# Modulation weights of the first norm in five groups instead of six, in one transformer-like layer on one core

## The chip, the cores and the metric

The kernel runs on one core of a Trainium2 chip. The metric is the device time of one execution in microseconds (us), lower is better. The kernel before takes 958.6 us, the median of three runs (958.38 to 959.06).

Engines are named as in the profile: PE (TensorE, matmuls; PEld is its weight load), DVE (VectorE), ACT (ScalarE), POOL (GpSimd) and SP (SyncE, which here only issues DMAs). A trailing q, as in SPq, means the engine's sequencer.

## The reference, cut to what matters

The program is one layer of a diffusion backbone in fp32: 512 latent tokens `x` and 256 context tokens `ctx`, width 1024. The layer's norms are modulated: a vector computed from the conditioning input `c` (for `x`) or `c_ctx` (for `ctx`) scales and shifts each of the 1024 channels.

```
sh1x, sc1x, ... = split(silu(c)     @ w_ada + b_ada, 6)
sh1c, sc1c, ... = split(silu(c_ctx) @ w_ada + b_ada, 6)
hc = rms_norm(ctx, norm1_g) * (1 + sc1c) + sh1c
hx = rms_norm(x,   norm1_g) * (1 + sc1x) + sh1x
z  = hx @ w_in                       # u, vs, q, r, ga, gb, k, v, lr
...
```

From `z` follow a spatial gating branch, a gated linear attention in both directions over the tokens, whose start states come from `hc`, a merge of both, and a convolutional feed-forward part with a second modulated norm. Only the beginning matters here: the shift and scale of the first norm (the first 2048 of the 6144 columns of `w_ada`, 8 MB), the normalised and modulated `hx`, and the first products with `w_in`.

## The kernel before

**Layout and number format.** The 1024 channels are eight tiles of 128, with the channel on the partition. Large products take an fp32 operand as two fp32r parts, a high part (`h`) and the remainder (`l`), and add three matmuls: high by high, high by low, low by high.

**The interleaved beginning.** At the start all data come from memory at once, and the kernel weaves three things together over the eight channel tiles k (the loop at L587):

- *The modulation.* The tiles are cut into groups: `GROUPS = (1, 1, 1, 1, 2, 2)` at L200, with `G0` the first tile of each. For a group, `ada_load(g)` (L210) loads the columns of `w_ada` for shift and scale as 256 KB transfers into tiles named `wa`: a one-tile group takes 4 of them, with 128 columns (512 B) in a run, a two-tile group 8, with 256 columns (1 KB) in a run. `ada_dot(g)` (L446, its matmuls at L455) multiplies them with the two activated condition vectors, 16 matmuls whatever the group's width, whose result DVE copies to `asb` (L602). `ada_sel(g)` (L459) turns the result to one column per channel with one small matmul per tile (L464) and makes scale `am` and shift `bm` with three short DVE operations (L467 to L469). `ada_mod(g)` (L471) applies them to the tiles of the group (L478) and splits each into `hxh` and `hxl`.
- *The first products.* `first_step(i, k, z)` (L523, matmul at L531): six outputs (q, k and four token tiles of v) times three part products, 18 matmuls per tile k. They need `hx[k]` and the rows of `w_in` that `first_load(i)` (L222) brings for two tiles at a time, 512 KB for v into a `raw` tile and two times 128 KB for q and k into `qkraw`. `first_split(i)` (L439) splits these: ACT casts the high parts (L441), DVE subtracts (L442). `first_split(1)` stands at the head of step k = 1, `first_split(2)` and `(3)` inside `ada_mod`, at tiles 4 and 6.
- *Small work*: after step 2 a transpose of `rows_b` to `vec_b` (L342) and `w2_stack` (L563, L566, L567), four DVE operations; after steps 3 and 7 a narrow product with `w_lr` (L513).

**Where the groups stand.** In the last step of a group's tiles the next group is made ready. The table `AT` (L586) gives, by the current group, before which third of the step's 18 matmuls `ada_dot` of the next group is issued; `ada_sel` and `ada_mod` follow one third later. With `AT = {0: 1, 1: 0, 2: 0, 3: 1, 4: 0}` the groups 1 to 5 are prepared in the steps 0, 1, 2, 3 and 5.

**What sets the order.** `in_order(START, nc.sync.engine)` (L241) fixes SP's issues to program order from the first load on: `x` (2 MB), then group and `first_load` calls as in L230 to L239, then the context tokens. `in_order(STRICT, ...)` (L635) does the same for PE, ACT and DVE through the whole beginning, so that each of them stalls at an instruction whose input isn't there. SP's DMAs take their semaphores in turn from a ring of eight (with the first few of ACT's), so that an issue waits until the one eight places before has landed.

**Buffers.** `heap` (44 tiles of 2 KB per partition) and `late` (27 of the same size) hold nearly everything. Group 3 and 4's `wa` tiles lie in `heap`, the others in `late` (L216).

**After the beginning** the weights are streamed by `weights()` (L191), split by ACT (L186) and DVE (L187), and multiplied, most at L281. The diff does not touch that part.

Of the kernel before, what the change touches and what calls it, by code (L numbers as in the profile page):

```python
# [16 lines left out]
P = 128  # L17
# [16 lines left out]
def backbone_kernel(  # L34
# [19 lines left out]
    def nm(s):  # L54
        cnt[0] += 1
        return f"{s}_{cnt[0]}"

    def heap(shape, dt=F32, s="h"):
        return hp.tile(shape, dt, tag="h", name=nm(s))

    def late(shape, dt=F32, s="l"):
        return lp.tile(shape, dt, tag="l", name=nm(s))
# [4 lines left out]
    def mm():  # L67
        return pm.tile([P, 512], F32, tag="mm", name=nm("mm"))

    def gl():  # L70
        return pg.tile([P, 512], F32, tag="gl", name=nm("gl"))
# [125 lines left out]

    GROUPS = (1, 1, 1, 1, 2, 2)  # L200
    NG = len(GROUPS)
    G0 = [sum(GROUPS[:i]) for i in range(NG)]
    fv = [tuple(wp.tile([P, 2, 512], dt, tag=tag, name=nm(tag), **kw)
# [6 lines left out]
    def ada_load(g):  # L210
        wa = []
        cg = GROUPS[g] * P
        nk = 512 // cg
        for kp in range(KT // nk):
            for kind in range(2):
                t_ = (heap if g in (3, 4) else late)([P, nk, cg], s="wa")  # L216
                c0 = kind * D + G0[g] * P
                dma(t_, w_ada[0, kp * nk * P:(kp + 1) * nk * P, c0:c0 + cg].rearrange("(k p) c -> p k c", p=P))  # L218
                wa.append(t_)
        return wa  # L220

    def first_load(i):  # L222
        rows = lambda c0, n: wi[2 * i * P:(2 * i + 2) * P, c0:c0 + n].rearrange("(k p) c -> p k c", p=P)
        dma(fv[i][0], rows(O_V, 512))
        raw = heap([P, 2, 2, P], s="qkraw")
        for j, c0 in enumerate((O_Q, O_K)):
            dma(raw[:, j], rows(c0, P))
        fqk.append((raw, late([P, 2, 2, P], F32R, s="qkh"), late([P, 2, 2, P], F32R, s="qkl")))

    was = {0: ada_load(0)}  # L230
    first_load(0)
    was[1] = ada_load(1)
    was[2] = ada_load(2)
    first_load(1)
    was[3] = ada_load(3)
    was[4] = ada_load(4)
    first_load(2)
    was[5] = ada_load(5)
    first_load(3)  # L239
    cin = tok_load(ctx[0], 2, late)  # L240
    in_order(START, nc.sync.engine)  # L241
# [204 lines left out]
    def ada_dot(g):  # L446

        cg = GROUPS[g] * P
        wa = was.pop(g)
        nk = 512 // cg  # L450
        aps = gl()
        for k in range(KT):
            for kind in range(2):
                j = kind + 2 * (k % 2)
                T.matmul(aps[32 * j:32 * j + 32, :cg], cs[:, k, :], wa[2 * (k // nk) + kind][:, k % nk, :],  # L455
                         start=(k < 2), stop=(k >= KT - 2), tile_position=(0, 32 * j))
        return [heap([P, cg], s="asb"), aps[:, :cg]]

    def ada_sel(g, asb):  # L459
        ng = GROUPS[g]  # L460
        k0 = G0[g]
        sel = gl()
        for b in range(ng):
            T.matmul(sel[:, b * 4:b * 4 + 4], asb[:, b * P:(b + 1) * P], selm, start=True, stop=True)  # L464
        sv = sel[:, :4 * ng].rearrange("p (b k r) -> p b k r", b=ng, k=2)
        ks = slice(k0, k0 + ng)
        V.tensor_tensor(am[:, ks, :], sv[:, :, 1, :], bsc1[:, ks].unsqueeze(2).to_broadcast([P, ng, 2]), op=ALU.add)  # L467
        V.tensor_tensor(am[:, ks, :], am[:, ks, :], n1g[:, ks].unsqueeze(2).to_broadcast([P, ng, 2]), op=ALU.mult)
        V.tensor_tensor(bm_[:, ks, :], sv[:, :, 0, :], bada[:, ks].unsqueeze(2).to_broadcast([P, ng, 2]), op=ALU.add)  # L469

    def ada_mod(g):  # L471
        k0 = G0[g]
        for k in range(k0, k0 + GROUPS[g]):
            f = fx[k]
# [108 lines left out]
    x_out(KT - 1, ps7, A.copy)  # L583
    lrx = heap([96, S], F32R, s="lrx")
    fps = [gl() for _ in range(2)] + [mm() for _ in range(4)]
    AT = {0: 1, 1: 0, 2: 0, 3: 1, 4: 0}  # L586
    for k in range(KT):  # L587
        g = max(i for i in range(NG) if G0[i] <= k)
        nxt = g + 1 if k == G0[g] + GROUPS[g] - 1 and g + 1 < NG else None
# [9 lines left out]
        for z in range(3):  # L599
            if nxt and z == AT[g]:  # L600
                dst, aps = ada_dot(nxt)
                V.tensor_copy(dst, aps)  # L602
            if nxt and z == AT[g] + 1:
                ada_sel(nxt, dst)
# [37 lines left out]
    for d in range(2):  # L642
        t_ = late([P, 4, P], s="pmask")
# [472 lines left out]
    for t in range(4):  # L1116
        row = []
        for hf in range(2):
            t_ = late([P, 512], s="x1")
# [92 lines left out]
    for hf in range(2):  # L1212
        t_ = late([P, 512], s="fng")
# [87 lines left out]
```

## Time and profile before

| what | value |
|---|---|
| median of three runs | 958.6 us (958.38 to 959.06) |
| the profiled execution's own time | 958.37 us |
| its span, first to last instruction | 956.7 us |
| PE / DVE / ACT / POOL busy | 934.7 / 653.3 / 350.9 / 13.4 us |
| granted TensorE clock, mean | 0.995 |
| DMA over the span | 111.95 MB, mean 117 GB/s |
| loads of `wa` | 32 in the beginning and 64 later, 256 KB each |

Times inside the profile are us from the first instruction. A timeline row has start, duration, engine, line, operation and operands (result <- inputs) and, in brackets, the idle time of the engine before it with what ended it. A row of waits says who waited for whom: us in total, how often, the longest. A row of windows has for a stretch of time the busy us of PE, PEld, DVE, ACT and POOL, with the instructions counted in brackets, then the clock granted to TensorE (1.00 is full), the DMA share and GB/s.

### The profile page before, as it was taken

What the parts mean: (1) busy time and instruction counts of PE and PEld (TensorE: products, weight loads), DVE (VectorE), ACT (ScalarE), POOL (GpSimd) and SP (SyncE); (2) the same over time, 40 slices, a digit from 0 to 9 for tenths busy, and PEclk for the clock granted to TensorE, in tenths of its full rate; (3) what the DMA queues carried; (4) which work ended last, traced back from release to release, by engine and by line L of the source; (5) the groups of instructions that cost most, each with busy time, mean ns of one, the idle gap of its engine ahead of it and who ended that gap; (6) DMA issues with size and microseconds to landing.
All of it is one profiled execution on the core that took longest, in us unless ns stands there. A gap on an engine that the chain in (4) does not pass through costs nothing.

```text
span 956.7 us, 12581 instructions
## 1 busy us (share of the span) xinstructions
PE 934.7 (98%) x4858; PEld 785.3 (82%) x4858; DVE 653.3 (68%) x1155; ACT 350.9 (37%) x593; POOL 13.4 (1%) x34
## 2 busy tenths in 40 slices
PE   6999999999999999999999999999999999999996
PEld 4676898988888888888878889988888888888885
DVE  5567768688699655597564357887777777893414
ACT  5136446566433222222222135433333333311313
POOL 3000000000000000000000000000000000000000
PEclk9999999999999999999999999999999999999998
DMA  9941311132147563683532433333333233232302
GB/s 274 334 127 30 111 45 53 36 111 67 32 124 220 167 206 89 210 275 98 158 97 88 161 109 111 110 89 91 108 89 110 88 92 108 73 119 74 111 0 88
DMA packets 147144, 111.95 MB, mean 117 GB/s; under 512 B 5849, under 2 KB 123941, under 8 KB 147085
## 3 DMA queue, kind: packets, MB, share of 16 engines
q1 hardware_dynamic: 145005, 109.72, 38.0%
q10 hardware_dynamic: 1728, 1.22, 0.4%
q8 instruction: 38, 0.62, 0.3%
q0 software_dynamic: 352, 0.22, 0.1%
q14 instruction: 21, 0.17, 0.1%
HBM read 109.04 MB, written 2.10 MB: 116 GB/s over the span
## 4 chain that ended last, share of the span: by engine, by line
PE 88%; DVE 5%; DMA 2%; SPq 2%; ACT 2%; issue 1%; DVEq 0%; ACTq 0%
PE mm L281 54%; PE gl L1224 7%; PE mm L1224 6%; PE mm L307 5%; PE gl L741 3%; PE mm L300 3%; PE mm L292 1%; PE mm L531 1%; PE gl L307 1%; PE mm L845 1%; DVE bc L709 1%; SPq L218 1%; PE gl L772 1%; PE gl L1040 1%; PE gl L531 1%
## 5 line engine op out<-in xcount | busy, mean ns | idle before, releaser
L186 ACT CAST wh<-raw 128x1024 fp32r<-128x1024 f32 x140 | 147.3, 1053 | 367.9 <-PE mm L281 247.3
L187 DVE TENSOR_TENSOR wl<-raw,wh 128x1024 fp32r<-128x1024 f32 x140 | 170.7, 1221 | 126.8 <-ACT wh L186 126.4
L281 PE MATMUL mm<-h2h,wh 128*128 128x512 f32 (+1 forms) x352 | 133.5, 379 | 0.0
L281 PE MATMUL mm<-h2l,wh 128*128 128x512 f32 (+1 forms) x352 | 133.5, 379 | 0.0
L281 PE MATMUL mm<-h2h,wl 128*128 128x512 f32 (+1 forms) x352 | 133.5, 379 | 0.0
L1191 DVE SCALAR_TENSOR_TENSOR cacc<-ca,ccol,cacc 128x441 f32<-128x441 f32 (+2 forms) x176 | 121.8, 695 | 4.6 <-ACT cacc L1185 0.5
L281 PE MATMUL mm<-hxh,wh 128*128 128x512 f32 x296 | 116.5, 393 | 0.0
L281 PE MATMUL mm<-hxh,wl 128*128 128x512 f32 x296 | 115.8, 391 | 0.0
L281 PE MATMUL mm<-hxl,wh 128*128 128x512 f32 x296 | 115.5, 390 | 0.0
L281 PEld LDWEIGHTS mm<-h2l,wh 128*128 128x128 f32 x352 | 66.2, 188 | 12.5
L281 PEld LDWEIGHTS mm<-h2h,wh 128*128 128x128 f32 x352 | 66.2, 188 | 12.5
L281 PEld LDWEIGHTS mm<-h2h,wl 128*128 128x128 f32 x352 | 66.2, 188 | 12.3
L281 PEld LDWEIGHTS mm<-hxh,wl 128*128 128x128 f32 x296 | 55.6, 188 | 11.7 <-issue 0.2
L281 PEld LDWEIGHTS mm<-hxh,wh 128*128 128x128 f32 x296 | 55.6, 188 | 11.5 <-issue 0.5
L281 PEld LDWEIGHTS mm<-hxl,wh 128*128 128x128 f32 x296 | 55.6, 188 | 11.2 <-issue 0.2
L1008 DVE SCALAR_TENSOR_TENSOR acc<-wa,cs,acc 128x512 f32<-128x512 f32 x64 | 45.7, 745 | 4.5 <-DMA wa<-in_w_ada_dram 4.5
L1224 PE MATMUL gl<-wh,gh 128*128 128x512 f32 (+1 forms) x110 | 40.5, 368 | 0.0
L1224 PE MATMUL gl<-wl,gh 128*128 128x512 f32 (+1 forms) x110 | 40.5, 368 | 0.0
L1224 PE MATMUL gl<-wh,gl 128*128 128x512 f32 (+1 forms) x110 | 40.5, 368 | 0.0
L1192 ACT ACTIVATE cacc<-cacc 128x512 f32<-128x512 f32 x22 | 13.9, 633 | 60.6 <-DVE cacc L1191 60.6
L1224 PE MATMUL mm<-wl,gh 128*128 128x512 f32 (+1 forms) x88 | 32.1, 365 | 0.0
L1224 PE MATMUL mm<-wh,gh 128*128 128x512 f32 (+1 forms) x88 | 32.0, 364 | 0.0
(363 smaller groups left out, 1740.8 us busy)
## 6 DMA issues: line engine op xcount, KB each, us to landing
raw<-in_w_in_dram SPq DMA_DIRECT2D x54, 512.0 KB, 4.0
wa<-in_w_ada_dram SPq DMA_DIRECT2D x96, 256.0 KB, 5.1
raw<-in_ffn_w_up_dram SPq DMA_DIRECT2D x44, 512.0 KB, 3.8
raw<-in_ffn_w_down_dram SPq DMA_DIRECT2D x22, 512.0 KB, 3.6
raw<-in_w_br_a_dram SPq DMA_DIRECT2D x8, 512.0 KB, 4.2
raw<-in_w_br_b_dram SPq DMA_DIRECT2D x8, 512.0 KB, 4.1
raw<-in_w_o_dram SPq DMA_DIRECT2D x8, 512.0 KB, 3.6
xin<-in_x_dram SPq DMA_DIRECT2D x8, 256.0 KB, 3.2
```

Of the source, the lines that this page charges most:

```text
L186: A.copy(wh, raw)
L187: V.tensor_tensor(wl, raw, wh.bitcast(F32), op=ALU.subtract)
L218: dma(t_, w_ada[0, kp * nk * P:(kp + 1) * nk * P, c0:c0 + cg].rearrange("(k p) c -> p k c", p=P))
L281: T.matmul(ps, a[:, k, :], b[:, c0:c0 + n], start=(k == 0 and i == 0), stop=(k == KT - 1 and i == 2))
L300: T.matmul(ps, a[:, t * P:(t + 1) * P], b[:, k % 4, :], start=(k == 0 and i == 0), stop=(k == KT - 1 and i == 2))
L307: T.matmul(ps, a[:, t * P:(t + 1) * P], b[:, k % 2, :], start=(k == 0 and i == 0), stop=(k == KT - 1 and i == 2))
L531: T.matmul(fps[i], a, b, start=(k == 0 and z == 0), stop=(k == KT - 1 and z == 2))
L741: T.matmul(ps, p_, q_, start=(start and z == 0), stop=(stop and z == 2))
L1008: V.scalar_tensor_tensor(acc[j], w_, cs[:, k, 0:1], acc[j], op0=ALU.mult, op1=ALU.add)
L1191: V.scalar_tensor_tensor(o, a_[:, r0 + dy:r1 + dy, c0 + dx:c1 + dx], wcol(tap), o, op0=ALU.mult, op1=ALU.add)
L1192: A.activation(acc, acc, AF.Gelu)
L1224: T.matmul(ps, a[:, t * P:(t + 1) * P], b[:, kk, c0:c0 + n], start=(first and i == 0), stop=(last and i == 2))
```

## The change

`GROUPS` becomes `(1, 1, 2, 2, 2)`: the former groups 2 and 3, one tile each, are one group of two tiles. The number of loads stays 32 with the same bytes; 8 loads have 256 columns in place of 128. SP's order follows: group 2 is now 8 transfers in place of 4 and stands ahead of `first_load(1)`, the next two-tile group ahead of `first_load(2)`, the last ahead of `first_load(3)`. `AT` loses an entry: the group of tiles 2 and 3 is prepared in step 1, that of tiles 4 and 5 in step 3 (before its first third, where it was its second), that of tiles 6 and 7 in step 5. The `wa` tiles of the new groups 2 and 4 lie in `heap`, of group 3 in `late`.

```diff
-    GROUPS = (1, 1, 1, 1, 2, 2)
+    GROUPS = (1, 1, 2, 2, 2)
...
-                t_ = (heap if g in (3, 4) else late)([P, nk, cg], s="wa")
+                t_ = (heap if g in (2, 4) else late)([P, nk, cg], s="wa")
...
     was[2] = ada_load(2)
     first_load(1)
     was[3] = ada_load(3)
+    first_load(2)
     was[4] = ada_load(4)
-    first_load(2)
-    was[5] = ada_load(5)
     first_load(3)
...
-    AT = {0: 1, 1: 0, 2: 0, 3: 1, 4: 0}
+    AT = {0: 1, 1: 0, 2: 0, 3: 0}
```

## The prediction

> **What bounds the kernel now.** I read the page's busy shares, then who TensorE (PE) waited for, then the first 80 us instruction by instruction, since all that the diff touches runs there.
>
> ```profile
> span 956.7 us, 12581 instructions
> ...
> PE 934.7 (98%) x4858; PEld 785.3 (82%) x4858; DVE 653.3 (68%) x1155; ACT 350.9 (37%) x593; POOL 13.4 (1%) x34
> ```
>
> PE is busy for 98% of the span. What does not shorten PE's own work or its waits does not show in the time. Its waits over the whole run, the longest ones and the only later one on a DMA:
>
> ```profile
> PE mm L342 <- DMA rows<-in_b_ada_dram: 6.0, 1, 6.0
> PE gl L531 <- ACT xT L424: 1.9, 1, 1.9
> PE gl L489 <- ACT hcf L498: 1.7, 1, 1.7
> ...
> PE gl L464 <- DVE asb L602: 0.6, 1, 0.6
> ...
> PE gl L1131 <- DMA crow<-in_ffn_conv_w_dram: 0.4, 1, 0.4
> ```
>
> PE never waits for a modulation weight (wa), though they fill the DMA for the first 50 us. The 0.6 us before L464 is a wait for the DVE copy L602, inside the stretch that changes. After it PE waits mostly for engines that PE itself feeds, so I carry any shift of the early stretch to the end one to one; the 0.4 us for crow is the most that a later transfer could absorb.
>
> Now PE's timeline over the six interleaved steps that matter (start, duration, line; a step is 18 matmuls of L531):
>
> ```profile
> 28.28 1.08 PE L455 MATMUL gl<-wa,cs 128*32 128x128 f32 x32
> 29.29 0.74 PE L531 MATMUL gl<-hxh,qkh 128*128 128x512 f32 x2
> ...
> 31.59 0.39 PE L464 MATMUL gl<-selm,asb 128*128 128x4 f32 x2 [0.62 <-DVE asb L602]
> ...
> 34.77 1.08 PE L455 MATMUL gl<-wa,cs 128*32 128x128 f32 x32
> ...
> 37.27 0.28 PE L464 MATMUL gl<-selm,asb 128*128 128x4 f32 x2
> ...
> 40.33 0.25 PE L342 MATMUL gl<-ident,rows 40*128 40x40 f32 x1
> 40.51 0.73 PE L531 MATMUL gl<-hxh,qkh 128*128 128x512 f32 x2
> ...
> 47.38 1.07 PE L513 MATMUL gl<-xT,w_lr 128*32 128x512 f32 x8
> 48.38 0.72 PE L531 MATMUL gl<-hxh,qkh 128*128 128x512 f32 x2
> ...
> 52.70 1.93 PE L455 MATMUL gl<-wa,cs 128*32 128x256 f32 x32
> ...
> 56.06 0.50 PE L464 MATMUL gl<-selm,asb 128*128 128x4 f32 x4
> ...
> 59.28 0.61 PE L531 MATMUL gl<-hxh,qkh 128*128 128x512 f32 x2
> ...
> 63.36 0.61 PE L531 MATMUL gl<-hxh,qkh 128*128 128x512 f32 x2
> ```
>
> L455 is a group's dot product, L464 its selection. Step 1 runs from 28.28 to 34.77, step 2 to 40.33, the transpose of vec_b to 40.51, step 3 to 47.38, the w_lr product to 48.38, where step 4 begins. PE has no idle time here but the 0.62 us.
>
> **The change part by part.** *PE work.* Prices are start to start. The plain step 6 takes 63.36 - 59.28 = 4.08 us. Step 2, with a one-tile group, takes 40.33 - 34.77 = 5.56: such a group costs 1.48. Step 5, with a two-tile group, takes 59.28 - 52.70 = 6.58: that costs 2.50. Two one-tile groups made into one save 2 x 1.48 - 2.50 = 0.46 us. Changed, step 1 holds a two-tile group (tiles 2 and 3), step 2 none, step 3 a two-tile group (tiles 4 and 5), which now stands in its first third and not its second, as step 5 has it. If nothing waits, the stretch becomes 6.58 + 4.08 + 0.18 + 6.58 + 1.00 = 18.42 us where it was 48.38 - 28.28 = 20.10: 1.68 us less. Of this 0.46 is the merging, 0.62 the wait, 0.29 step 3's order (6.87 against 6.58) and the rest step 1's restart after its wait.
>
> *What now comes late.* Group 2's loads double, and the queue still has first_load(1) (1 x 512 KB and 2 x 128 KB) behind them: 1,024 KB more stand ahead of it. Its landing is awaited at the head of step 1, by first_split(1). These are ACT's and DVE's rows there:
>
> ```profile
> 28.51 0.62 ACT L441 CAST qkh<-qkraw 128x512 fp32r<-128x512 f32 x1 [6.88 <-DMA qkraw<-in_w_in_dram]
> 29.03 1.04 ACT L441 CAST wh<-raw 128x1024 fp32r<-128x1024 f32 x1
> ```
>
> ```profile
> 31.25 0.28 DVE L602 COPY asb<-gl 128x128 f32<-128x128 f32 x1
> ...
> 42.43 0.68 DVE L567 TENSOR_TENSOR w2s<-w2r,w2s 32x512 fp32r<-32x512 f32 x1
> 44.10 0.42 DVE L602 COPY asb<-gl 128x256 f32<-128x256 f32 x1 [0.99 <-PE gl L455]
> ```
>
> ACT had been idle for 6.88 us when the raw tile landed at 28.5. Then follow ACT's two casts, DVE's two subtractions, and only behind them, since each engine keeps its program order, the copy of the dot product at 31.25, which the selection at 31.59 waits for. So the 0.62 us is really a wait for first_load(1): 28.51 to 31.59 is a fixed chain of 3.08 us, and 3.22 with the copy of a two-tile group (0.42 against 0.28). Nothing hides it, because PE's queue holds the rest of step 1 behind the selection.
>
> How much later the tile lands depends on the rate:
>
> ```profile
> 15.00:20.00 5.00, 3.10 (x38) 2.04 (x29) 2.99 (x9) 2.71 (x5) 1.96 (x4) 1.00 1.18 296
> ...
> 25.00:30.00 5.00, 5.00 (x51) 3.83 (x48) 3.04 (x8) 1.49 (x2) 0.00 (x0) 0.89 1.05 291
> 30.00:35.00 5.00, 4.38 (x27) 3.07 (x29) 3.48 (x8) 0.07 (x1) 0.00 (x0) 1.00 1.01 320
> 35.00:40.00 5.00, 5.00 (x51) 4.10 (x44) 2.35 (x7) 0.00 (x0) 0.00 (x0) 1.00 1.09 357
> ...
> 75.00:80.00 5.00, 4.96 (x26) 4.20 (x27) 4.54 (x9) 3.30 (x7) 0.00 (x0) 1.00 0.02 3
> ```
>
> The last column is GB/s. Up to 30 us mostly 128-column groups move, in runs of 512 B: 291 to 296. From 30 to 40 mostly 256-column groups, in runs of 1 KB: 320 to 357. Group 2 and first_load(1) are 1,792 KB or 1.835 MB before: at 296 they take 6.2 us, so group 1 had landed at 28.5 - 6.2 = 22.3. Changed they are 2,816 KB or 2.884 MB: at 340, between the two later rows, 8.5 us, so the landing is at 30.8 (30.4 at 357, 31.3 at 320). That is 2.3 us later, between 1.9 and 2.8. [...]
>
> The selection then starts at 30.8 + 3.22 = 34.0. PE would have been ready at 28.28 + (56.06 - 52.70) = 31.64, so it stands for 2.4 us. From the selection to the end of step 1 is 3.22 (56.06 to 59.28) and 0.12 for restarting (34.77 - 31.59 against 40.33 - 37.27); then 4.08 + 0.18 + 6.58 + 1.00. Step 4 begins at 49.2, against 48.38: **0.8 us later** (0.4 to 1.3), so the wait eats the 1.68 us and half as much again.
>
> *What does not matter.* The next two-tile group needs as many bytes ahead of it as before, and its dot product stands near 41.8 instead of 42.1, with no DMA wait then; the last group and first_load(3) have the same bytes ahead too. Step 3's copy now follows the w2_stack work, whose last piece ends at 43.11, 2.78 us after vec_b's transpose; with 0.42 + 0.06 more it is ready at 3.26 us, and PE asks for it at 0.18 + 3.36 = 3.54. So 0.28 us cover it; without them it would cost up to what is missing. Heap and late tiles only swap places; the DMA count stays 32.
>
> *The clock.* A stop of over 2 us may cost more than itself:
>
> ```profile
> 21.19 0.50 PE L531 MATMUL gl<-hxh,qkh 128*128 128x512 f32 x1 [1.89 <-ACT xT L424]
> ...
> 23.20 1.94 PE L455 MATMUL gl<-wa,cs 128*32 128x128 f32 x32
> 25.06 1.68 PE L531 MATMUL mm<-wh,hxl 128*128 128x512 f32 x4
> ...
> 75.03 0.65 PE L489 MATMUL gl<-ident,xin 128*128 128x128 f32 x4 [1.73 <-ACT hcf L498]
> ```
>
> ```profile
> 22.00:23.00 1.00, 1.00 (x5) 0.86 1.20 297
> 23.00:24.00 1.00, 1.00 (x17) 0.50 1.06 320
> ...
> 26.00:27.00 1.00, 1.00 (x6) 0.93 1.15 319
> ```
>
> After the 1.89 us stop the granted clock was 0.50 for 0.28 + 3 + 0.14 = 3.42 us. The same dot product that takes 1.01 us to its successor at 28.28 took 25.06 - 23.20 = 1.86, so a cold stretch loses 0.46 of its 3.42 us: 1.57. After the 1.73 us stop the clock stayed at 1.00 (row of 75 to 80). The new stop of 2.4 us, of which about 2.2 would be recorded as idle (before, a start at 31.59 and not at 28.28 + 37.27 - 34.77 = 30.78, so 0.81 of delay, left 0.62), lies beyond the stop that did cost the clock, but there is one instance on each side. I take 1.4 us for a cold stretch, since part of it may fall into the stop itself (1.1 to 1.6).
>
> **Forecast.** 0.8 + 1.4 = 2.2 us slower: the profiled execution's own 958.4 becomes 960.6, and the median of 958.6, 0.2 above it, 960.8. What a measurement of this kernel can tell from no change is about 0.2%, or 1.9 us, so this lies just past that edge.
>
> **The rivals.**
> *The stop stays, the clock doesn't drop*: 0.8 us slower, 959.4, within 0.2%. For it: the 1.73 us stop cost no clock. Against it: the 1.89 us one did. [...]
> *The wider runs outpace the doubling*: the first two-tile group and first_load(1) land early enough that the saved PE work wins. It breaks even when step 4 starts at 48.38, so with first_load(1) at 30.0: 2.884 MB in 7.7 us, 375 GB/s. At no wait at all the kernel ends 1.68 us sooner, 956.9, and that needs 28.4, so 473 GB/s. No row of these slices is above 357, but group 1's landing at 22.3 is inferred, and half a microsecond there is as good as 20 GB/s.
> *The runs of 1 KB move no faster* (then the higher rates after 30 us come from something else, such as the 2 KB runs of first_load in between): 2.884 MB at 296 take 9.7 us, the landing is at 32.0, 1.2 us beyond my value, so the end is 2.0 us later without and 3.4 with the cold stretch: 962.0.
> *The change doesn't do what it says*: the 8 loads of group 2, now in heap tiles, could be held up in SyncE's queue for a free tile. At that point 8 xin, 1 qkraw and 8 wa tiles are asked of 44, so I give it nothing of its own.
>
> **How the numbers follow.** Stop with the clock drop 0.50, stop without 0.28, early landing 0.14 (a 0.04 part of it beyond 1.9 us, where something later must help), 1 KB runs no faster 0.08. Slower by over 0.2%: two thirds of the first, whose terms reach from 0.4 + 1.1 to 1.3 + 1.6, and nearly all of the last: 0.40. Faster by over 0.2%: 0.04. Within: 0.56. The range takes in all of the first two, the upper part of the early landings and the last up to its value: 958.3 to 962.0.
>
> **What would show it.** Right: in the changed profile the selection of group 2 (L464) carries a wait of about 2.2 us put down to the copy L602, starting near 34.0; ACT's first cast of first_split(1) starts near 30.8 after a DMA; 16 fewer L455 matmuls (32 records); step 2 takes about 4.1 us; the clock is 0.50 for some 3.4 us between 33 and 40. Wrong: a cast before 29.5, a DMA wait at L455, a wait in step 3's selection, or a shift at step 4 that is not found at the end.

## The result and the profile after

The changed kernel takes 960.94 us (median of 19 runs, 958.64 to 963.31), the kernel before beside it 959.0 (19 runs, 957.56 to 961.75). The ratio is 1.0021, with a 95% interval of 1.0014 to 1.0029: about 2 us slower. The profiled execution took 961.71 us, 3.3 more than that of before. The first lines of its page, and the longest waits of PE:

```profile
span 959.7 us, 12507 instructions
...
PE 934.0 (97%) x4826; PEld 785.2 (82%) x4826; DVE 652.2 (68%) x1150; ACT 351.5 (37%) x594; POOL 13.6 (1%) x34
```

```profile
PE mm L341 <- DMA rows<-in_b_ada_dram: 6.2, 1, 6.2
PE gl L463 <- DVE asb L601: 3.2, 1, 3.2
PE gl L530 <- ACT xT L423: 1.9, 1, 1.9
PE gl L488 <- ACT hcf L497: 1.7, 1, 1.7
PE gl L1130 <- DMA crow<-in_ffn_conv_w_dram: 1.7, 1, 1.7
```

Line numbers below L238 have moved up by one. PE has 32 records fewer, and is busy 0.7 us less while the span is 3.0 longer (each of the two profiles has one stretch of 3.4 us at half clock while PE works): what was added is waiting. Two rows have grown: the wait for the copy of the dot product, 0.6 to 3.2, and the one for crow, 0.4 to 1.7. PE's timeline where the first of them lies (the group at 35.12 takes 1.91 us at half clock; the same four matmuls take 1.09 at 32.38 in the kernel before):

```profile
26.80 1.93 PE L454 MATMUL gl<-wa,cs 128*32 128x256 f32 x32
...
33.57 0.70 PE L463 MATMUL gl<-selm,asb 128*128 128x4 f32 x4 [3.25 <-DVE asb L601]
...
35.12 1.91 PE L530 MATMUL mm<-wh,hxl 128*128 128x512 f32 x4
...
38.46 0.61 PE L530 MATMUL gl<-hxh,qkh 128*128 128x512 f32 x2
...
42.63 0.25 PE L341 MATMUL gl<-ident,rows 40*128 40x40 f32 x1
42.81 1.93 PE L454 MATMUL gl<-wa,cs 128*32 128x256 f32 x32
...
49.44 1.06 PE L512 MATMUL gl<-xT,w_lr 128*32 128x512 f32 x8
50.43 0.73 PE L530 MATMUL gl<-hxh,qkh 128*128 128x512 f32 x2
```

ACT's first cast of first_split(1) and DVE's copy behind it:

```profile
30.36 0.62 ACT L440 CAST qkh<-qkraw 128x512 fp32r<-128x512 f32 x1 [8.70 <-DMA qkraw<-in_w_in_dram]
```

```profile
33.10 0.42 DVE L601 COPY asb<-gl 128x256 f32<-128x256 f32 x1
```

The raw tile lands at 30.4, the copy starts 2.74 us later, the selection at 33.57, and PE has stood still for 3.25 us by then. Read alone, the row of waits blames DVE; only ACT's row shows that a transfer is behind it. The granted clock (third column from the right) at the end of the stop, in rows that count PE alone, and the rates (last column) of the loads:

```profile
33.00:34.00 1.00, 0.43 (x4) 0.97 1.10 349
34.00:35.00 1.00, 1.00 (x4) 0.50 1.08 372
35.00:36.00 1.00, 1.00 (x4) 0.50 1.09 354
...
37.00:38.00 1.00, 1.00 (x5) 0.82 1.10 342
```

```profile
15.00:20.00 5.00, 3.24 (x46) 2.44 (x46) 3.03 (x10) 2.83 (x5) 0.00 (x0) 1.00 1.18 304
20.00:25.00 5.00, 3.78 (x43) 2.87 (x44) 2.67 (x5) 1.66 (x4) 0.00 (x0) 1.00 1.10 345
25.00:30.00 5.00, 5.00 (x48) 3.23 (x46) 2.06 (x6) 0.00 (x0) 0.00 (x0) 1.00 1.10 350
```

From 20 to 30 us, where group 2's wider runs now move, the rate is 345 to 350 GB/s; it was 291 from 25 to 30 before. Step 4 starts at 50.43 against 48.38: 2.05 us later. Of the 3.0 us by which this span is longer, some 1.3 more come at crow (1.7 against 0.4), and the tail behind PE's last matmul gives 0.3 back.

### The profile page after: what moved, and what is told of

Same layout as the page of the kernel before. It is cut to its first block, busy times and chain, and to the rows that moved or that the text cites. A ratio compares the mean times of both kernels' runs of the same rounds, so it can differ in the third digit from the quotient of the medians.

```text
span 959.7 us, 12507 instructions
## 1 busy us (share of the span) xinstructions
PE 934.0 (97%) x4826; PEld 785.2 (82%) x4826; DVE 652.2 (68%) x1150; ACT 351.5 (37%) x594; POOL 13.6 (1%) x34
## 4 chain that ended last, share of the span: by engine, by line
PE 86%; DVE 6%; DMA 3%; ACT 1%; SPq 1%; issue 1%; DVEq 0%; ACTq 0%
PE mm L280 53%; PE gl L1223 7%; PE mm L1223 6%; PE mm L306 5%; PE gl L740 3%; PE mm L299 3%; PE mm L291 1%; PE mm L530 1%; PE gl L306 1%; DMA wa<-in_w_ada_dram 1%; PE mm L844 1%; DVE bc L708 1%; DVE vsn L968 1%; PE gl L771 1%; PE gl L530 1%
```

## The experiments

Theory A is the prediction's: first_load(1) lands late, PE stops, and the stop brings a half clock. Theory B is what the first profile leaves possible: the stop is made good, and the time is lost at the crow loads near 554 us. Rival C is that fewer, wider groups are slower in themselves. Every kernel was timed beside the kernel before on the same chip; the first four shared one set, the next four a second, two a third; the last two, made for one wait, were run once. In the first set the kernel before had 958.26 us, in the second 958.87, in the third 958.93.

**The changed kernel again**, with no edit.

> The changed kernel again, for a second profile beside the first, which put 1.29 us of its 3.0 us into a longer wait for the crow transfer near 554 us. Theory A (the late first_load(1) stops PE for 2.2 to 3.3 us in step 1, and the stop brings 3.4 us of half clock): the stop and the half clock are there again, the crow wait is anything from 0.3 to 1.7, and the median is 1.4 to 2.4 us above the kernel before. Theory B (the stop is harmless, the time is lost at crow): the crow wait is near 1.7 again and at least 1 us longer than before.

Measured: 960.75 us, ratio 1.0026 (1.0017 to 1.0036), so 2.5 us above the kernel before, a little more than A's upper figure. Its profile:

```profile
PE gl L463 <- DVE asb L601: 2.7, 1, 2.7
...
PE gl L1130 <- DMA crow<-in_ffn_conv_w_dram: 1.5, 1, 1.5
```

```profile
33.00:34.00 1.00, 0.98 (x6) 1.00 1.09 351
34.00:35.00 1.00, 1.00 (x4) 0.53 1.07 371
...
37.00:38.00 1.00, 1.00 (x5) 0.76 1.10 340
```

Stop and half clock are there again, but crow too has a long wait again, so this run alone doesn't decide between A and B.

**Subtractions later.** The casts stay at the head of step 1; DVE's two subtractions go into `ada_mod(2)`, behind tile 2, so that the copy of the dot product no longer stands behind them. Loads and groups stay.

```diff
-    def first_split(i):
-        for raw, wh, wl in (fqk[i], fv[i]):
-            A.copy(wh, raw)
-            V.tensor_tensor(wl, raw, wh.bitcast(F32), op=ALU.subtract)
+    def first_cast(i):
+        for raw, wh, wl in (fqk[i], fv[i]):
+            A.copy(wh, raw)
+    def first_sub(i):
+        for raw, wh, wl in (fqk[i], fv[i]):
+            V.tensor_tensor(wl, raw, wh.bitcast(F32), op=ALU.subtract)
+    def first_split(i):
+        first_cast(i)
+        first_sub(i)
...
             if k in (4, 6):
                 first_split(k // 2)
+            if k == 2:
+                first_sub(1)
...
         if k == 1:
-            first_split(1)
+            first_cast(1)
```

> DVE's two subtractions of first_split(1) stand behind the modulation of tile 2 and no longer ahead of the copy of group 2's dot product; ACT's casts, the loads and the groups stay. Theory A: the selection of group 2 has no wait above 0.2 us, the clock stays at 1.00 after it, step 4 starts at 45.2 to 46.9 (50.4 in the changed kernel), and the median is 3.2 to 5 us below the changed kernel, 1.4 to 3 us below the kernel before. Theory B: step 4 starts earlier too, but the end comes at most 1 us earlier than the changed kernel's, since it is crow that counts. Rival C (fewer, wider groups are slower in themselves): no faster than the kernel before.

Measured: 957.40 us, 3.35 below the changed kernel and 0.86 below the kernel before (ratio 0.9985, 0.9976 to 0.9994, which is 0.6 to 2.3 us). Its PE timeline:

```profile
28.70 1.93 PE L461 MATMUL gl<-wa,cs 128*32 128x256 f32 x32
...
32.06 0.50 PE L470 MATMUL gl<-selm,asb 128*128 128x4 f32 x4
...
47.26 0.73 PE L539 MATMUL gl<-hxh,qkh 128*128 128x512 f32 x2
```

No wait stands at 32.06, and no half clock follows (1.00 from 30 to 40 us). Though the transfer lands no earlier (ACT's cast starts at 30.9), the stop and all that hung on it are gone. B allowed 1 us at the end; 3.35 came, with a crow wait of 0.9. C said that five groups would be no faster than the kernel before, and these are faster; but the same edit also speeds up six groups (below), so this run alone doesn't rule C out. Against the kernel before the gain of 0.86 us is under the 1.4 to 3 that A said, only the upper part of its interval reaches there, and step 4 is 0.4 us outside: this execution had the early half clock (the four matmuls at 23.13 took 1.91 us), and the changed kernel's two profiles did not (1.09 and 1.07 at 22.02 and 22.07).

**The stop filled.** Matmuls without use write into the tile that the selection then overwrites.

```diff
         sel = gl()
+        if g == 2:
+            for _ in range(5):
+                T.matmul(sel[:, :256], ones, ident.unsqueeze(1).to_broadcast([P, 2, P]), start=True, stop=True)
         for b in range(ng):
```

> Five extra fp32 matmuls without use, of 256 columns and about 0.45 us each, fill PE's stop ahead of the selection of group 2; the stop's end is still set by first_load(1). Theory A: recorded idle there falls under 1.2 us, the granted clock stays at 1.00 from 30 to 45 us, the selection starts at 33.5 to 34.3 as before, step 4 starts near 49.2 to 49.8, and the median is 0.9 to 1.5 us below the changed kernel. If the half clock costs nothing, or comes for another reason: the same as the changed kernel or up to 0.5 us slower.

Measured: 959.62 us, 1.13 below the changed kernel (ratio to before 1.0008, 0.9999 to 1.0017).

```profile
28.61 1.93 PE L454 MATMUL gl<-wa,cs 128*32 128x256 f32 x32
...
31.97 2.32 PE L464 MATMUL gl<-ident,ones 128*128 128x256 f32 x10
34.12 0.51 PE L466 MATMUL gl<-selm,asb 128*128 128x4 f32 x4
...
49.29 0.73 PE L533 MATMUL gl<-hxh,qkh 128*128 128x512 f32 x2
```

```profile
30.00:35.00 5.00, 5.00 (x34) 4.02 (x27) 2.55 (x6) 1.57 (x2) 0.00 (x0) 1.00 1.10 354
35.00:40.00 5.00, 5.00 (x23) 4.13 (x22) 2.91 (x7) 1.97 (x3) 0.00 (x0) 1.00 1.12 345
```

The selection starts 0.5 us later than in the changed kernel's first profile, and yet step 4 starts 1.1 us sooner (0.6 sooner than in its second): the clock stays at 1.00. From the selection to step 4 it takes 15.17 us here and 16.86 in both profiles of the changed kernel. This tells the clock's share, 1.1 us in the medians and 1.7 between the profiles, apart from that of the stop. That the filler kept the clock up is read from the medians, whose intervals against the kernel before only touch (1.0017); this profile alone doesn't show it: it had the early half clock (the four matmuls at 23.02 took 1.91 us), so PE came late to the selection and would have stood for some 1.6 us without the filler (from 31.97 to the cast at 30.38 plus the chain of 3.22). Whether the half clock follows a stop of that length here, no profile of the changed kernel shows.

**first_load(1) ahead of group 2** in the queue.

```diff
-    was[2] = ada_load(2)
     first_load(1)
+    was[2] = ada_load(2)
```

> first_load(1) stands ahead of the doubled group 2 in the queue. Theory A: ACT's first cast of first_split(1) starts near 25 to 26.5 and no longer ends a wait, but group 2 itself now lands near 30.4, so the wait moves from the selection to the dot product; step 1 ends about 1 us sooner than in the changed kernel, the stop is split or shorter, and the median is 0.8 to 2.4 us below the changed kernel (the more if the clock does not drop). If the load order is not the cause: no change.

Measured: 958.57 us, 2.18 below the changed kernel (ratio to before 0.9999, 0.9991 to 1.0008).

```profile
28.40 2.80 PE L454 MATMUL gl<-wa,cs 128*32 128x256 f32 x32
...
32.62 0.50 PE L463 MATMUL gl<-selm,asb 128*128 128x4 f32 x4
```

The cast starts at 23.5 (earlier than expected), step 1 ends 2.6 us sooner than in the changed kernel where about 1 was expected (35.84 against 38.46), and the dot product takes 2.80 instead of 1.93 us; I put these 0.87 us down to its last pieces, though no row of waits names them, and no half clock follows (1.00 from 25 to 40 us). The same bytes in another order bring most of the loss back.

**Six groups, group 3 loaded ahead of first_load(1).** This puts the change's 1,024 KB into the kernel before.

```diff
-    first_load(1)
     was[3] = ada_load(3)
+    first_load(1)
```

> The kernel before with six groups, only that the 1,024 KB of group 3 stand ahead of first_load(1) in the queue: the change's effect on the queue alone, without its wider group. Theory A: ACT's first cast of first_split(1) starts near 32.0 (28.5 before, 1.05 MB at 296 GB/s later), the selection of group 2 near 35.1, PE stops there for 3.5 to 5 us, the clock falls to 0.50 behind it, and the median is 3.5 to 5 us above the kernel before. If the wider group or its place in the step is what costs: no change.

Measured: 964.09 us, 5.2 above the kernel before (ratio 1.0049, 1.0035 to 1.0062, so 3.4 to 5.9 us).

```profile
31.43 0.62 ACT L441 CAST qkh<-qkraw 128x512 fp32r<-128x512 f32 x1 [9.15 <-DMA qkraw<-in_w_in_dram]
```

```profile
34.51 0.39 PE L464 MATMUL gl<-selm,asb 128*128 128x4 f32 x2 [2.92 <-DVE asb L602]
```

```profile
20.00:25.00 5.00, 3.16 (x8) 2.05 (x8) 2.99 (x5) 2.27 (x5) 0.00 (x0) 0.70 1.20 286
25.00:30.00 5.00, 5.00 (x78) 3.86 (x77) 2.34 (x7) 0.00 (x0) 0.00 (x0) 0.96 1.06 288
...
35.00:40.00 5.00, 5.00 (x40) 3.65 (x43) 1.99 (x6) 0.24 (x1) 0.00 (x0) 0.66 1.10 348
```

The queue alone makes the stop, the half clock and the loss, without a wider group. The cast is 0.6 us earlier and the stop shorter than expected, the median a little above the expected 3.5 to 5. The rows from 20 to 30 us also tell what the wider runs do: here the weights of tiles 2 and 3 move in 512 B runs, in the same place of the queue where the changed kernel moves them in 1 KB runs, at 286 to 288 GB/s and not at 345 to 350.

**Six groups, subtractions later.** The diff is that of the second experiment, made in the kernel before.

> The kernel before with six groups, DVE's subtractions of first_split(1) behind the modulation of tile 2. Neither this nor the five groups with the same edit waits for first_load(1), so the two differ by the groups alone. Theory A: the 0.62 us before group 2's selection is gone, the median is 0.5 to 1.5 us below the kernel before, and the five groups with the same edit are 0.5 to 1.1 us below this one (0.46 for the merging, 0.29 for step 3's order). If wider groups are slower in themselves: this one is the faster of the two.

Measured: 957.64 us, 1.23 below the kernel before (ratio 0.9989, 0.9978 to 0.9999), and the wait is gone. The five groups with the same edit had 0.9985 in another set, where 0.5 to 1.1 us less was expected: the intervals overlap, and the order of the two medians stays open here. Between the two profiles, from group 2's dot product to step 4, five groups take 18.56 us and six 19.20.

**Crow first, then an early filler.** Both build on the five groups with later subtractions. The first moves the three crow loads ahead of the x1 loads; the second also fills PE's stops near 18 to 21 us, writing into the first output before its first real matmul.

```diff
+    crow = [late([110, P], s="crow") for _ in range(2)]
+    cw = ffn_conv_w[0].rearrange("a b (f p) -> (a b f) p", p=P)
+    dma(crow[0], cw[0:110])
+    dma(crow[1][0:88, :], cw[110:198])
+    dma(crow[1][88:110, :], r8(ffn_conv_b[0]))
     x1 = []
...
     fps = [gl() for _ in range(2)] + [mm() for _ in range(4)]
+    for _ in range(6):
+        T.matmul(fps[0][:, :256], ones, ident.unsqueeze(1).to_broadcast([P, 2, P]), start=True, stop=True)
```

> Five groups with the later subtractions, and besides the three small crow loads ahead of the eight x1 loads near 545 us. The crow wait near 554 was 0.4 to 1.7 us in six profiles. Expected: under 0.2 us, the median 0.4 to 1.5 us below the kernel without this edit.

> As the one with crow first, and besides six fp32 matmuls without use ahead of step 0, where PE stops for 0.7 and 1.9 us near 18 to 21 us and the half clock follows in most profiles. If the half clock is lost work: the clock stays at 1.00 from 10 us on, group 2's dot product starts near 26.8 to 27.2 (28.7 with the later subtractions alone), step 4 near 45 to 46, and the median is 0.9 to 1.7 us lower than without the filler. If something else (the landing of group 2 near 28) then binds: under 0.5 us lower, with a DMA wait at the dot product.

Measured with crow first: 956.86 us, ratio 0.9974 (0.9965 to 0.9984), a crow wait of 0.2 us (0.2 to 0.4 in the four profiles with this edit, where under 0.2 was expected). That is 0.5 below the kernel without this edit, but in another set, and the intervals overlap: likely, not shown. With the filler as well: 955.34, ratio 0.9959 (0.9946 to 0.9972), 1.52 below in the same set.

```profile
18.36 2.86 PE L595 MATMUL gl<-ident,ones 128*128 128x256 f32 x12
...
26.82 1.93 PE L461 MATMUL gl<-wa,cs 128*32 128x256 f32 x32
...
45.38 0.73 PE L539 MATMUL gl<-hxh,qkh 128*128 128x512 f32 x2
```

```profile
20.00:25.00 5.00, 5.00 (x50) 3.76 (x49) 2.71 (x5) 1.70 (x4) 0.00 (x0) 1.00 1.10 347
```

With the filler the clock was 1.00 from 20 to 25, group 2's dot product starts at 26.82 and not at 28.70, and nothing later takes the gain back.

**Six and five groups with all three edits**, in one set, so that only the groups differ.

> Six groups as before, with the three other edits: later subtractions, crow first, early filler. With neither first_load(1) nor the clock in the way, it differs from the five groups with the same edits by the groups alone. By the steps' prices five groups are 0.5 to 0.8 us faster (0.64 from step 1 to step 4 between the profiles of the two kernels with later subtractions). If the wider runs or fewer groups bring nothing of themselves: within 0.2 us of each other.

> The five groups with the three edits again, beside six groups with the same on the same chip: 0.5 to 0.8 us below them, 3.3 to 4.5 us below the kernel before.

Measured: six groups 955.79 us (954.71 to 956.19), five groups 954.90 (954.75 to 955.73); ratios to the kernel before 0.9963 (0.9950 to 0.9976) and 0.9956 (0.9943 to 0.9969). These rows are the start of group 2's dot product and of step 4, six groups first:

```profile
27.20 1.08 PE L462 MATMUL gl<-wa,cs 128*32 128x128 f32 x32
...
46.39 0.72 PE L540 MATMUL gl<-hxh,qkh 128*128 128x512 f32 x2
```

```profile
26.36 2.06 PE L461 MATMUL gl<-wa,cs 128*32 128x256 f32 x32
...
45.04 0.73 PE L539 MATMUL gl<-hxh,qkh 128*128 128x512 f32 x2
```

From one to the other it takes 19.19 us with six groups and 18.68 with five. The profile shows the grouping's own gain as 0.51 us, 0.13 of it taken back by a dot product stretched to 2.06; the medians differ by 0.89, a little more than expected, but the runs of the two overlap, and the intervals against the kernel before are too wide to confirm so little. Rival C, that five groups are slower in themselves, falls with this pair. The five groups with all three edits have the lowest medians of the study (954.90, and 955.34 in the set before), 4.0 us below the kernel before in this set and some 6 below the changed one.

**The kernel before, twice more**, with no edit, for the wait at crow.

> The kernel before again, for its wait at crow. In three profiles of six groups with the crow loads in their place it was 0.3 to 0.6 us, in five profiles of five groups 0.4 to 1.7. If five groups lengthen it: 0.3 to 0.6 again. If it varies by itself: over 0.8 as likely as not.

> The kernel before once more, with the same two readings: 0.3 to 0.6 us at crow if five groups lengthen the wait, over 0.8 as likely as not if it varies by itself.

Measured: 958.50 and 958.86 us in one execution each. The first:

```profile
30.80 0.38 PE L464 MATMUL gl<-selm,asb 128*128 128x4 f32 x2 [1.98 <-DVE asb L602]
...
47.58 0.72 PE L531 MATMUL gl<-hxh,qkh 128*128 128x512 f32 x2
```

```profile
PE gl L1015 <- DVE accl L274: 0.8, 1, 0.8
PE gl L1131 <- DMA crow<-in_ffn_conv_w_dram: 0.4, 1, 0.4
```

The second:

```profile
47.98 0.72 PE L531 MATMUL gl<-hxh,qkh 128*128 128x512 f32 x2
```

```profile
PE gl L1131 <- DMA crow<-in_ffn_conv_w_dram: 0.3, 1, 0.3
```

With these, five profiles of six groups have 0.3 to 0.6 us at crow, five of five groups 0.4, 0.9, 1.4, 1.5 and 1.7. Only one lies in the others' band, so the five groups very likely lengthen this wait, by some 0.8 us on the mean. Why is open. It is not a net loss of 0.8 us, though: three of the five profiles of six groups, both of these among them, wait 0.8 to 0.9 us at L1015, a little earlier in the program, and none of the five groups does. From step 4 to the first matmul on crow, six groups take 504.0 to 505.4 us and five 504.6 to 505.8, which is 0.3 us apart on the means. The first of the two profiles also shows the kernel before without the early half clock (the four matmuls at 21.38 took 1.08 us): PE is there sooner, waits 1.98 us for the same transfer, and step 4 starts at 47.58, with no half clock behind the stop (the four at 31.60 took 1.08).

## Why the prediction was right

The mechanism and its two terms held, and the measured 960.94 us is 0.14 from the forecast. That it came so close is partly luck: the kernel before stood at 959.0 us beside it and not at 958.6, and the sum knew nothing of the longer wait at crow. The difference, which is what the sum forecast, was 2.2 us; it measured 1.9 and 2.5 in the two sets. The ratios, 1.0021 and 1.0026, lie just past the edge of 0.2%, to which I had given a chance of 0.40, against 0.56 for staying within it.

*PE's work*: forecast 18.42 us from group 2's dot product to step 4 if nothing waits; 18.56 in the kernel with later subtractions. Step 1 with its two-tile group took 6.59 us there, as step 5 had before (6.58). So the merging does save (0.5 to 0.6 us in the profiles, where 0.46 + 0.29 = 0.75 were reckoned), and the change is slower for another reason.

*The landing*: forecast 30.8 (30.4 to 31.3); the cast started at 30.36, and at 29.8 to 30.9 in the other profiles of five groups with this load order. The size that was a little off is the rate, 340 GB/s forecast, 345 to 350 measured. The cast of the first profile before, at 28.51, was the latest of five with six groups and the old load order (27.7 to 28.5): on the means of the profiles the cast moved from 28.0 to 30.3, 2.3 us later as forecast. The rival of runs that move no faster falls, since the same bytes at the same place moved at 286 to 288 GB/s in 512 B runs and at 345 to 350 in 1 KB runs.

*The chain behind it*: 3.22 us forecast, 33.57 - 30.36 = 3.21 measured.

*The stop*: about 2.2 us of idle time forecast, 3.25 and 2.67 measured. The step that was off is PE's readiness at 31.64, counted from a dot product that starts at 28.28. In both profiles of the changed kernel the early half clock (22.7 to 26.1 us in the kernel before) had not come, and the dot product started at 26.8. This left the sum untouched, since the end of the stop hangs on the transfer alone; but it made the half clock after the stop likelier than the 0.50 I gave it.

*The clock*: forecast 1.4 us. From the selection to the end of step 1 it took 38.46 - 33.57 = 4.89 us where 3.34 was reckoned at full clock and 3.20 measured with the filler, so 1.6 to 1.7 were lost in this profile; the filler won back 1.13 in the medians. The rival without a clock drop falls: stops of 2.67, 2.92 and 3.25 us all brought one, while that of 1.98 in the kernel before did not.

*The sum and the end*: step 4 starts at 48.38, 47.58 and 47.98 in the three profiles of the kernel before and at 50.43 and 49.88 in the two of the changed one, 2.2 us apart on the means, which is the forecast. That such a shift reaches the end is shown by all fourteen profiled executions: step 4 starts between 45.0 and 52.9 us, and from there to the end each takes between 909.5 and 911.3. Something is added, though: the wait at crow, which I had bounded by 0.4 us, grew to 1.5 and 1.7. From step 4 to the end the changed kernel's two profiles take 0.4 us more than the three of the kernel before (911.0 against 910.6 on the means), and 2.2 and 0.4 make 2.6 where the medians show 1.9 and 2.5; the last half microsecond of the account stays open. Theory B is wrong as to the main loss, but the end of the program holds a small part of the difference that the prediction did not have.

## What to carry to other kernels

A wait names the engine that came last, not the cause: follow the queue of that engine back until something was idle for long, here ACT with 8.70 us before a DMA. Merging small pieces saved work on the bound engine (0.5 to 0.6 us here), but where transfers stand in one queue ask which unrelated load now has more bytes ahead of it, and what stands behind its first user in the engine's program order; moving two subtractions out of the way was worth more (3.35 us) than the merging. The changed kernel's stops of PE of 2.67 and 3.25 us cost up to 1.7 us beyond their length, and idle time that can't be avoided was cheaper filled in both places tried here, by 1.13 and 1.52 us in the medians.

## What the runs showed of the hardware

The half clocks of the beginning lasted 3.4 us wherever the length was measured: from 22.72 to 26.14 us in the kernel before, one in each profile of the changed kernel, one with first_load(1) ahead, and two in the six groups with group 3 loaded ahead, the first from 22.0 us on and the second between 35 and 40. Such a stretch came after stops shorter than that: 1.89 us with 0.69 shortly before it, or 2.67 alone, but not after 1.98 alone. After the same pair of stops near 18 to 21 us it came in seven of the eleven profiles that leave them open, so it depends on something besides the stop's length; what that is, these runs don't show. In six of the seven the first matmul behind the stop was slow already (0.67 to 0.80 us, and 0.50 to 0.51 in the other five profiles), in the kernel before the clock fell at 22.72. There it also falls at 951.2 us, with PE's last matmul over at 949.2.

The ten runs of the five groups with all three edits, in two sets, lie between 954.27 and 955.73 us, while the kernel before spreads from 957.17 to 961.47 beside them.
